# A chain of chunks in two accumulator banks, its outputs stored over its values, and two-operand GpSimd work given to other engines, in a one-core hybrid layer (RWKV-7, mLSTM, mixture of experts)

## The chip, the cores and the metric

The kernel runs on one core of a Trainium2 chip. The metric is the device time of one execution in microseconds (us). The engines are called by the profile's names: PE (TensorE matmul, with PEld for its weight loads), DVE (VectorE), ACT (ScalarE), POOL (GpSimd) and SP, which here only issues DMAs. The accumulators that PE writes lie in eight banks of 512 float32 values per partition; the program holds them as one tile, `accs`.

## The reference, cut to what matters

One decoder layer over 528 tokens (16 meta tokens and 512 others), width 1024, all in float32.

1. RMS norm of the input, then one projection to 3,080 columns.
2. Half of the heads: RWKV-7 time mixing. Per head a 64x64 state S is carried over the tokens: `S = S * d_t + (S a_t) b_t^T + v_t k_t^T`, `y_t = S r_t`. Then a norm per head, a bonus term and a gate.
3. The other half: an mLSTM, chunked over time, with a causal convolution on q and k.
4. Output projection and residual, RMS norm, a router (one of 4 groups, then 2 of its 8 experts), 32 SwiGLU experts of 1024 -> 2x512 -> 1024, residual, final RMS norm.

## The kernel before, in words

**Start (lines 505 to 640).** The transposed input `xT` arrives in eight blocks of 128 x 528. Each block is split by ACT and DVE in a high and a low part (`xh`, `xl`), so that three fast matmuls stand for one float32 matmul. The sum of squares for the first norm is made by `squares` (L613): even blocks are squared on ACT, odd ones on DVE, and POOL adds each to `acc`. Two float32 matmuls with a matrix of ones then sum `acc` over the partitions (`pss`).

**Mixing stage.** A planner (`Weave`) runs a set of Python generators, each with a rank, against a simple model of the engines' times, and so fixes the order of PE's and SP's instructions; the order of the other engines' instructions comes from the compiler. PE, like the others, takes its instructions strictly in that order. A generator can give way to another only where it has a `yield`. `projections` (L1008) is the filler with a low rank: it streams 24 weight blocks, each split in two by `prepare` (L671) and `split_block`. `heads` (L836) builds, for each of four pairs of RWKV heads, the decayed keys and queries; `products` (L902) multiplies them per chunk of 64 tokens; `inverse0` (L1357) and `inverse` (L1372) solve small triangular systems step by step (`interleaved`, L1335: one multiplication and one addition per step or half step), the first on POOL, the second on DVE.

**The chain of chunks (L1476).** Nine steps carry the RWKV state: one of 16 tokens and eight of 64. In a step, `removals` (L1421) writes `pW`, DVE copies it to `Wt`; `solved` (L1437) multiplies `Wt` by the solved system into `uv`, for each half p of the 128 partitions four matmuls and then a copy (ACT for p = 0, DVE for p = 1); `next_state` (L1446) writes `pS`, and DVE adds the decayed state, once for each p; `outputs` (L1460) writes `yv` in two groups of matmuls, the second group for each p four matmuls and then a copy by ACT into `yT`. `solved` and `outputs` hold no `yield`; the one behind `next_state` leads straight back to the chain, whose rank 0 goes before all fillers, so that the matmuls of `outputs` stand right behind those of `next_state` in PE's queue. Each of these blocks is 4 x 64 columns wide. The chain holds four banks: `pU` (banks 4 and 5: `uv` for p = 0 and `pW` in one, `uv` for p = 1 and `pS` in the other) and `pY` (banks 6 and 7: `yv` for p = 0 in one, for p = 1 in the other). All other generators share banks 0 to 3 (`every`) until the chain ends.

**After the chain.** `variances`, `gate_a` and `outputs_a` with `gated` (L1576) finish the RWKV outputs; the space of the tiles `E`, free only when the chain has ended, takes the output weights; `mixer` (L1861) does the output projection and the router. From the mark `var` on, `prefetch` (L1950) loads expert weights into whatever space is free.

**Experts (from L2040).** Sixteen pairs of experts, 12.6 MB of weights a pair, streamed by SP's queue through all free space; PE's order is written out by hand.

Of the kernel before, what the change touches and what calls it, by code (L numbers as in the profile page):

```python
# [17 lines left out]
L = 528  # L18
# [417 lines left out]
def layer(ctx, tc, a, out, dbg=None, stop=None):  # L436
# [145 lines left out]
    acc = A.get([128, L], name="acc")  # L582
# [29 lines left out]
    A.put(idle_)  # L612
    def squares(k):  # L613
        sq = A.get([128, L], name="sq") if k else acc
        if k % 2:
            V.tensor_tensor(sq, xT[:, k], xT[:, k], op=OP.mult)
        else:
            S.activation(sq, xT[:, k], AF.Square)
        if k:
            G.tensor_tensor(acc, acc, sq, op=OP.add)  # L620
            A.put(sq)

    first_block(0, 2)
    for k in range(8):
# [10 lines left out]
        if k >= 2:  # L635
            proj_k(pk1, k1h, k1l, k)
            squares(k - 2)
    for k in range(6, 8):
        squares(k)

# [27 lines left out]
    def late():  # L668
        return len(every) == 8

    def prepare(kind):  # L671

        lo_by = V if late() and kind != "q" or "P3" not in W.marks else G
# [19 lines left out]
    pss = B.get(2, "pss", rest)  # L693
    for h in range(2):
        P.matmul(pss[:, h, :264], m("ones"), acc[:, 264 * h:264 * h + 264], start=True, stop=True)
# [4 lines left out]
    A.put(xT, acc)  # L700
# [135 lines left out]
    def heads():  # L836

        for j in range(4):
# [5 lines left out]
            G.tensor_tensor(MV[:, :, 128:192], i64[:, None].to_broadcast([128, 8, 64]),  # L844
                            DT[:, j, 1:9][:, :, None].to_broadcast([128, 8, 64]), op=OP.mult)
            G.tensor_scalar(mv0[:, NM:], i64, DT[:, j, 0:1], 0.0, op0=OP.mult, op1=OP.add)
            G.tensor_tensor(nk, nk, al, op=OP.mult)
            kp = al
            S.activation(kp, al, AF.Identity, scale=c("k_a", j), bias=dv[:, 12 + j:13 + j])
            G.tensor_tensor(kp, kp, kx[j], op=OP.mult)  # L850
# [13 lines left out]
            for p in range(2):  # L864
                for i in range(2):
                    (S.copy if p else gcopy)(E[i][PAR[p], :, j, p], MV[PAR[p], 4 * i:4 * i + 4, 0:128])
            G.tensor_scalar(r[:, NM:], r[:, NM:], c("r_k", j), 0.0, op0=OP.mult, op1=OP.add)
            G.tensor_tensor(r[:, NM:], r[:, NM:], kp[:, NM:], op=OP.mult)
# [322 lines left out]
    def states():  # L1191
# [3 lines left out]
        for tb in range(-1, 3):  # L1195
# [6 lines left out]
            kw = A.get([128, 4, 64], name="kw")  # L1202
# [154 lines left out]
    def inverse0():  # L1357
# [8 lines left out]
        yield from interleaved(G, XL0, lambda s: NL0[:, s + 1:, s], NM, tm0, 99)  # L1366
# [5 lines left out]
    def inverse():  # L1372
# [39 lines left out]
        A.put(NL, XL, Y1, Y2, *tmps, *Zs)  # L1412
        dump("X", Bt)
# [23 lines left out]
    def solved(ch, first, vu, n):  # L1437
        for p in range(2):
            for j in range(4):
                o = slice(64 * p, 64 * p + n)  # L1440
                P.matmul(uv[o, p, j], (X0[PAR[p], j] if first else Bt[PAR[p], ch, j, 0:64]), Wt[PAR[p], j],
                         start=True, stop=True)
            o = slice(64 * p, 64 * p + n)
            (V.tensor_copy if p else S.copy)(vu[o, :, p], uv[o, p])
# [15 lines left out]
    def outputs(ch, vs, vu):  # L1460
        if ch % 2 == 0:
            yT.append(A.get([128, 4, 128], name="yT"))
        for j in range(4):
            for p in range(2):
                P.matmul(yv[PAR[p], p, j], vs[:, j, p], E[ch // 4][:, ch % 4, j, p, 64:128], start=(j == 0),
                         stop=False, skip_group_check=True)
        for p in range(2):
            for j in range(4):
                P.matmul(yv[PAR[p], p, j], vu[PAR[p], j, p], Bt[PAR[p], ch, j, 64:128], start=False,
                         stop=(j == 3), skip_group_check=True)  # L1470
            last = S.copy(yT[ch // 2][PAR[p], :, 64 * (ch % 2):64 * (ch % 2) + 64], yv[PAR[p], p])
# [4 lines left out]
    def chain():  # L1476
# [853 lines left out]
```

## Time and profile before

| | |
|---|---|
| median of 3 runs | 911.82 us (910.79 to 916.01) |
| the profiled execution's own time | 910.37 us |
| its span, first to last instruction | 908.5 us |
| mean granted clock of PE, share of full speed | 0.956 |
| busy: PE / DVE / ACT / POOL | 843.5 / 434.4 / 270.9 / 226.4 us |
| HBM read | 234 MB, 263 GB/s over the span |

The span is the time from the first to the last instruction on the core; the 1.9 us by which the execution's own time is longer lie around it. Busy shares are means over stages with quite different limits, so the stages have to be read one by one.

### The profile page before, as it was taken

To read this page: it belongs to the slowest core of one execution; us is meant where nothing else is said; L and a number is where in the kernel's file an instruction comes from. 1 tells how busy PE (TensorE), PEld (TensorE's weight loads), DVE (VectorE), ACT (ScalarE), POOL (GpSimd) and SP (SyncE) were. 2 spreads that over 40 slices of the span, in tenths; PEclk is the share of its full clock that TensorE was granted. 3 is DMA by queue.
4 is the path that set the end of the run, shared out by engine and by line. 5 is a ranking of instruction groups with operands and counts; after the bars stand their busy time and mean duration, and the time that the engine had idled before them with its cause. 6 is when DMAs were issued, how large, how long until landed. Compare 5 with 4: busy or idle time off the path is not lost.

```text
span 908.5 us, 13524 instructions
## 1 busy us (share of the span) xinstructions
PE 843.5 (93%) x5385; PEld 522.1 (57%) x5386; DVE 434.4 (48%) x822; ACT 270.9 (30%) x522; POOL 226.4 (25%) x297
## 2 busy tenths in 40 slices
PE   7989889879999997998899999999999999989994
PEld 5878778769999776887334444334444333323331
DVE  7676766995544668327213334233334133322324
ACT  5666555434435773333101110011101011001102
POOL 6064544464545156254100000000000000000002
PEclk8989999987999999998899999999999999999998
DMA  7201123111100137929899999999999999999982
GB/s 237 71 3 46 47 69 83 47 47 53 51 25 25 48 107 291 403 71 335 335 402 419 420 420 420 421 420 420 420 419 421 420 421 420 420 421 421 420 341 96
DMA packets 45141, 235.56 MB, mean 259 GB/s; under 512 B 9906, under 2 KB 10290, under 8 KB 21008
## 3 DMA queue, kind: packets, MB, share of 16 engines
q1 hardware_dynamic: 42192, 228.56, 63.3%
q0 software_dynamic: 2160, 3.93, 1.2%
q10 hardware_dynamic: 720, 2.15, 0.6%
q8 instruction: 44, 0.72, 0.3%
q14 instruction: 25, 0.20, 0.1%
HBM read 234.36 MB, written 4.19 MB: 263 GB/s over the span
## 4 chain that ended last, share of the span: by engine, by line
PE 53%; DMA 24%; DVE 13%; ACT 4%; issue 2%; POOL 2%; SPq 0%; ACTq 0%; DVEq 0%; POOLq 0%
PE accs L304 25%; PE accs L2070 14%; DVE arF L304 8%; DMA arF<-wgu 7%; PE accs L2115 6%; DMA arF<-wdn 5%; DMA arM<-wgu 4%; ACT arF L304 3%; PE accs L1993 2%; DMA arH<-wgu 2%; DMA arN<-wgu 2%; DMA arN<-wdn 2%; PE accs L1994 2%; DMA arF<-wo 1%; POOL arF L304 1%
## 5 line engine op out<-in xcount | busy, mean ns | idle before, releaser
L304 PE MATMUL accs<-arS,arR 128*128 128x264 f32 (+2 forms) x1136 | 184.5, 314 | 10.2 <-DVE arR L304 5.0
L304 PEld LDWEIGHTS accs<-arS,arR 128*128 128x128 f32 (+1 forms) x1136 | 162.4, 200 | 22.5 <-DVE arR L304 5.5
L304 PE MATMUL accs<-arF 64*64 64x64 f32 (+18 forms) x1223 | 127.7, 268 | 27.5 <-DVE arF L304 17.4
L1996 DVE TENSOR_TENSOR arF<-arF,accs 128x512 f32<-128x512 f32 x124 | 80.7, 681 | 98.1 <-PE accs L1994 96.6
L304 PEld LDWEIGHTS accs<-arF 128*128 128x128 f32 (+7 forms) x1202 | 102.2, 157 | 37.3 <-DVE arF L304 11.4
L2070 PE MATMUL accs<-arF 128*64 128x512 f32 x488 | 116.4, 608 | 4.2 <-DMA arF<-wgu 4.2
L304 POOL TENSOR_TENSOR arF<-arF 128x528 f32<-128x528 f32 (+13 forms) x101 | 92.3, 917 | 67.6 <-DVE arF L304 45.4
L1804 POOL DMA_INDIRECT arM<-hd,arF x15 | 15.2, 1012 | 376.2 <-DVE arF L1794 362.7
L304 DVE TENSOR_TENSOR arF<-arF 64x16 f32<-64x16 f32 (+33 forms) x183 | 89.5, 535 | 5.1 <-POOL arF L304 2.8
L2092 ACT ACTIVATE arF<-accs,arF 128x512 f32<-128x512 f32 x16 | 11.0, 687 | 247.5 <-PE accs L2070 247.5
L2070 PEld LDWEIGHTS accs<-arF 128*64 128x64 f32 x488 | 32.6, 138 | 74.2 <-issue 57.5
L304 ACT ACTIVATE arF<-arF 128x528 f32<-128x528 f32 (+8 forms) x108 | 57.9, 559 | 49.8 <-DVE arF L304 35.5
L2125 DVE SCALAR_TENSOR_TENSOR arO<-accs,arF,arO 128x1024 fp32r<-128x1024 f32 x15 | 19.3, 1283 | 103.6 <-ACT arO L2124 103.6
L304 POOL TENSOR_SCALAR arF<-arF 64x256 f32<-64x256 f32 (+9 forms) x97 | 55.3, 572 | 42.6 <-ACT arF L304 19.6
L2115 PE MATMUL accs<-arF 128*64 128x512 f32 x280 | 62.3, 595 | 0.5 <-issue 0.5
L304 ACT COPY arF<-accs 64x256 f32<-64x256 f32 (+6 forms) x119 | 43.2, 370 | 64.1 <-PE accs L304 30.5
L1993 PE MATMUL accs<-arO,OHT 128*128 128x512 f32 x124 | 57.4, 463 | 0.0
L304 DVE TENSOR_TENSOR arF<-accs,arF 128x528 f32<-128x528 f32 (+7 forms) x81 | 35.4, 460 | 34.1 <-PE accs L304 20.6
L1994 PE MATMUL accs<-arO,OHT 128*128 128x512 f32 x124 | 48.9, 394 | 0.0
L2070 PE MATMUL accs<-arN,arF 128*64 128x512 f32 x200 | 47.1, 599 | 1.6 <-DMA arN<-wgu 1.6
L304 PE MATMUL accs<-arW,arS 128*128 128x512 f32 x192 | 47.8, 406 | 0.0
L2070 PE MATMUL accs<-arM,arF 128*64 128x512 f32 x200 | 46.7, 599 | 1.0 <-DMA arM<-wgu 0.9
(141 smaller groups left out, 932.6 us busy)
## 6 DMA issues: line engine op xcount, KB each, us to landing
arF<-wgu SPq DMA_DIRECT2D x61, 1024.0 KB, 19.8
arF<-wdn SPq DMA_DIRECT2D x35, 1024.0 KB, 20.1
arN<-wgu SPq DMA_DIRECT2D x25, 1024.0 KB, 19.9
arM<-wgu SPq DMA_DIRECT2D x25, 1024.0 KB, 19.8
arH<-wgu SPq DMA_DIRECT2D x16, 1024.0 KB, 19.9
arN<-wdn SPq DMA_DIRECT2D x15, 1024.0 KB, 19.9
arF<-wb SPq DMA_DIRECT2D x23, 512.0 KB, 3.6
arH<-wdn SPq DMA_DIRECT2D x5, 1024.0 KB, 19.8
```

The lines of the kernel that those rows point to most:

```text
L304: r = f(*args, **kw)
L1804: nc.gpsimd.indirect_dma_start(out=xt[p % 2], out_offset=None, in_=hd, in_offset=bass.IndirectOffsetOnAxis(ap=idx[:, p % 2:p % 2 + 1], axi ...
L1993: P.matmul(pq, lhs, oh[:, hs], start=True, stop=False)
L1994: P.matmul(pq, lhs, ol[:, hs], start=False, stop=True)
L1996: V.tensor_tensor(hv, hv, pq, op=OP.add)
L2070: P.matmul(pgu[64 * e:64 * e + 64, h], x[:, k, 64 * e:64 * e + 64], w[:, D * e + 512 * h:D * e + 512 * h + 512], start=(k == 0), stop=(k = ...
L2092: S.activation(av, pgu[:, 0], AF.Silu, scale=r1_)
L2115: P.matmul(pdn[64 * e:64 * e + 64, h], aT[:, k, 64 * e:64 * e + 64], w[:, D * h + 512 * e:D * h + 512 * e + 512], start=(k == 0), stop=(k ...
L2125: V.scalar_tensor_tensor(ol, pdf, g1_, oh.bitcast(F32), op0=OP.mult, op1=OP.subtract)
```

## The change

- **Start.** Each block's squares go to a tile of their own, all on ACT; DVE adds them in pairs; the float32 matmul with ones sums the four pair tiles in the accumulator (8 matmuls in place of 2). POOL has no part in it.
- **`heads`.** Three POOL multiplications of two tensors for each pair of heads go to DVE; POOL's scaling of `r` and its multiplication become one DVE instruction; two POOL copies into `E` go to ACT.
- **`inverse0`** runs its steps on DVE. **`prepare`** leaves the low parts of the split weights to DVE until the inverse is done (before: until the mark `P3`, then POOL), to POOL during the chain as before, to DVE after it.
- **The chain** has two banks: `uv` of both halves and `pW` in one, `pS` and `yv` of both halves in the other. The two banks that come free go to `every` at the chain's start. `yT` lies over the values `Vs` of its two chunks.
- **After the chain**, the first multiplication of `gated` goes from POOL to DVE; the tile `sqs` becomes four; `kw`, `Gw` and `sqs` wait for space where they had to find it.
- On POOL stay: the multiplications in `valued`, `conv`, `after_o`, `next_state`'s decay `SD`, half of the output weights' splits, and the copies of `values`.

```diff
     def squares(k):
-        sq = A.get([128, L], name="sq") if k else acc
+        sqs2.append(A.get([128, L], name="sq"))
+        S.activation(sqs2[k], xT[:, k], AF.Square)
         if k % 2:
-            V.tensor_tensor(sq, xT[:, k], xT[:, k], op=OP.mult)
-        else:
-            S.activation(sq, xT[:, k], AF.Square)
-        if k:
-            G.tensor_tensor(acc, acc, sq, op=OP.add)
-            A.put(sq)
+            V.tensor_tensor(sqs2[k], sqs2[k], sqs2[k - 1], op=OP.add)
+
+    def summed(k):
+        for h in range(2):
+            P.matmul(pss[:, h, :264], m("ones"), sqs2[k][:, 264 * h:264 * h + 264], start=(k == 1), stop=(k == 7))
...
-        lo_by = V if late() and kind != "q" or "P3" not in W.marks else G
+        lo_by = V if late() and kind != "q" or "inverse" not in W.marks else G
...
-            G.tensor_tensor(MV[:, :, 128:192], i64[:, None].to_broadcast([128, 8, 64]),
+            V.tensor_tensor(MV[:, :, 128:192], i64[:, None].to_broadcast([128, 8, 64]),
                             DT[:, j, 1:9][:, :, None].to_broadcast([128, 8, 64]), op=OP.mult)
...
-            G.tensor_tensor(nk, nk, al, op=OP.mult)
+            V.tensor_tensor(nk, nk, al, op=OP.mult)
...
-            G.tensor_tensor(kp, kp, kx[j], op=OP.mult)
+            V.tensor_tensor(kp, kp, kx[j], op=OP.mult)
...
-                    (S.copy if p else gcopy)(E[i][PAR[p], :, j, p], MV[PAR[p], 4 * i:4 * i + 4, 0:128])
-            G.tensor_scalar(r[:, NM:], r[:, NM:], c("r_k", j), 0.0, op0=OP.mult, op1=OP.add)
-            G.tensor_tensor(r[:, NM:], r[:, NM:], kp[:, NM:], op=OP.mult)
+                    S.copy(E[i][PAR[p], :, j, p], MV[PAR[p], 4 * i:4 * i + 4, 0:128])
+            V.scalar_tensor_tensor(r[:, NM:], r[:, NM:], c("r_k", j), kp[:, NM:], op0=OP.mult, op1=OP.mult)
...
-        yield from interleaved(G, XL0, lambda s: NL0[:, s + 1:, s], NM, tm0, 99)
+        yield from interleaved(V, XL0, lambda s: NL0[:, s + 1:, s], NM, tm0, 99)
...
-                P.matmul(uv[o, p, j], (X0[PAR[p], j] if first else Bt[PAR[p], ch, j, 0:64]), Wt[PAR[p], j],
+                P.matmul(uv[o, j], (X0[PAR[p], j] if first else Bt[PAR[p], ch, j, 0:64]), Wt[PAR[p], j],
                          start=True, stop=True)
             o = slice(64 * p, 64 * p + n)
-            (V.tensor_copy if p else S.copy)(vu[o, :, p], uv[o, p])
+            (V.tensor_copy if p else S.copy)(vu[o, :, p], uv[o])
...
-            yT.append(A.get([128, 4, 128], name="yT"))
+            yT.append(Vs[:, ch:ch + 2].rearrange("p c j x -> p (c j x)").rearrange("p (j t) -> p j t", j=4))
...
-                P.matmul(yv[PAR[p], p, j], vs[:, j, p], E[ch // 4][:, ch % 4, j, p, 64:128], start=(j == 0),
+                P.matmul(yv[PAR[p], j], vs[:, j, p], E[ch // 4][:, ch % 4, j, p, 64:128], start=(j == 0),
...
-                P.matmul(yv[PAR[p], p, j], vu[PAR[p], j, p], Bt[PAR[p], ch, j, 64:128], start=False,
+                P.matmul(yv[PAR[p], j], vu[PAR[p], j, p], Bt[PAR[p], ch, j, 64:128], start=False,
                          stop=(j == 3), skip_group_check=True)
-            last = S.copy(yT[ch // 2][PAR[p], :, 64 * (ch % 2):64 * (ch % 2) + 64], yv[PAR[p], p])
+            last = S.copy(yT[ch // 2][PAR[p], :, 64 * (ch % 2):64 * (ch % 2) + 64], yv[PAR[p]])
...
-        pY = yield from bank(2, "pY", wide)
-        pW, pS = (pU[:, i, 256:512].rearrange("p (j x) -> p j x", j=4) for i in range(2))
-        uv = pU[:, :, 0:256].rearrange("p a (j x) -> p a j x", j=4)
-        yv = pY[:, :, 0:256].rearrange("p a (j x) -> p a j x", j=4)
+        (uv, pW), (pS, yv) = ([pU[:, i, 256 * h:256 * h + 256].rearrange("p (j x) -> p j x", j=4) for h in range(2)]
+                              for i in range(2))
         yield from until(*(f"V{j}" for j in range(4)), "P3", "X0")
+        every.extend(wide)
...
-        A.put(Vs, *VS, *VU, Wt, SD, DT)
-        Gw = A.get([128, 4, T], name="Gw")
-        sqs.append(A.get([128, 4, 4, 128], name="sq"))
-        B.put(pU, pY)
-        every.extend(rest)
+        A.put(*VS, *VU, Wt, SD, DT)
+        B.put(pU)
+        Gw, = yield from W.room(A, 1, [128, 4, T], F32, "Gw")
+        sqs.extend((yield from W.room(A, 4, [128, 4, 128], F32, "sq")))
+        every.extend(small)
...
-        G.tensor_tensor(y, y, Gw[:, :, 128 * tb:128 * tb + 128], op=OP.mult)
+        V.tensor_tensor(y, y, Gw[:, :, 128 * tb:128 * tb + 128], op=OP.mult)
```

## Rows read from the trace of the kernel before

**Rows 1.** Stages: stretch, its length, busy time by engine (count), PEclk, DMA.
```profile
50.00:165.00 115.00, 100.41 (x659) 92.43 (x659) 82.12 (x123) 65.27 (x129) 57.36 (x88) 0.94 0.19 54
165.00:194.00 29.00, 20.81 (x154) 19.79 (x152) 28.56 (x69) 9.67 (x23) 17.31 (x28) 0.93 0.18 55
194.00:225.00 31.00, 30.75 (x369) 29.50 (x370) 23.09 (x59) 13.91 (x26) 17.63 (x24) 0.72 0.08 24
225.00:300.00 75.00, 75.00 (x971) 68.80 (x970) 35.18 (x66) 32.75 (x67) 35.99 (x50) 0.96 0.12 37
300.00:351.00 51.00, 44.96 (x293) 34.56 (x290) 38.50 (x61) 34.67 (x87) 27.44 (x20) 0.99 0.32 100
656.00:861.00 205.00, 197.47 (x972) 73.99 (x970) 64.50 (x114) 20.82 (x28) 5.95 (x6) 1.00 1.01 420
```

**Rows 2.** Chain that ended last, in order of time: start, us, what.
```profile
194.25 103.05 PE accs L304 x1307
...
840.83 19.81 DMA arM<-wgu
```

**Rows 3.** Timeline of the start: start, us, engine, operation, tiles, shapes, count.
```profile
8.02 1.88 POOL L304 TENSOR_TENSOR arF<-arF 128x528 f32<-128x528 f32 x1 [4.53 <-ACT arS L304]
8.66 1.81 DVE L304 SCALAR_TENSOR_TENSOR arS<-arF,arS 128x528 fp32r<-128x528 f32 x1
17.44 0.79 DVE L304 SCALAR_TENSOR_TENSOR arS<-arF,arS 128x528 fp32r<-128x528 f32 x1
25.72 1.05 PE L304 MATMUL accs<-arF 128*128 128x264 f32 x4
```

**Rows 4.** Timeline of the inverse, 167.2 to 167.3.
```profile
167.18 2.40 POOL L304 TENSOR_TENSOR arR<-arF,arR 128x1024 fp32r<-128x1024 f32 x1 [2.43 <-ACT arR L304]
167.22 2.60 DVE L304 TENSOR_TENSOR arF<-arF 128x135 f32<-128x135 f32 x1
```

**Rows 5.** Groups by form on DVE, 0 to 230: busy, mean ns, idle before.
```profile
L304 DVE TENSOR_TENSOR arF<-arF 128x512 f32<-128x512 f32 x6 | 4.0, 686 | 0.1
L304 DVE TENSOR_TENSOR arF<-arF 128x1024 f32<-128x1024 f32 x3 | 3.7, 1222 | 0.1
L304 DVE TENSOR_TENSOR arF<-arF 128x30 f32<-128x30 f32 x4 | 0.5, 188 | 0.0
```

**Rows 6.** Groups by form on POOL, 0 to 440.
```profile
L304 POOL TENSOR_TENSOR arF<-arF 128x512 f32<-128x512 f32 x20 | 29.8, 1501 | 16.8 <-DVE arF L304 11.1 <-ACT arF L304 4.0 <-PE accs L304 1.1
L304 POOL TENSOR_TENSOR arR<-arF,arR 128x1024 fp32r<-128x1024 f32 x8 | 19.4, 2423 | 25.0 <-ACT arR L304 24.9
```

**Rows 7.** Timeline of PE: three of its waits (in brackets: idle before, releaser).
```profile
66.66 0.40 PE L304 MATMUL accs<-arF 128*128 128x192 f32 x1 [3.29 <-POOL arF L304]
194.25 0.58 PE L304 MATMUL accs<-arF 128*128 128x128 f32 x1 [6.00 <-DVE arF L304]
350.61 0.80 PE L304 MATMUL accs<-arS,arR 128*128 128x512 f32 x1 [5.03 <-DVE arR L304]
```

**Rows 8.** Timeline of DVE and ACT reading the accumulators.
```profile
74.71 0.37 ACT L304 COPY arF<-accs 64x256 f32<-64x256 f32 x1 [1.26 <-DVE arE L304]
75.11 1.41 DVE L304 TENSOR_TENSOR arE<-accs,arF 64x512 f32<-64x512 f32 x2 [0.43 <-ACT arF L304]
228.01 0.41 DVE L304 COPY arF<-accs 16x256 f32<-16x256 f32 x1 [3.02 <-PE accs L304]
228.51 0.36 ACT L304 COPY arF<-accs 16x256 f32<-16x256 f32 x1 [5.25 <-DVE arF L304]
231.60 0.36 ACT L304 COPY arF<-accs 16x256 f32<-16x256 f32 x1 [0.55 <-PE accs L304]
231.85 0.42 DVE L304 COPY arF<-accs 16x256 f32<-16x256 f32 x1 [3.43 <-PE accs L304]
```

**Rows 9.** Timeline of one step of the chain, on PE, DVE and ACT.
```profile
266.89 0.27 PE L304 MATMUL accs<-arE,arF 128*64 128x64 f32 x1
267.39 0.88 DVE L304 TENSOR_TENSOR arF<-accs,arF 64x256 f32<-64x256 f32 x2 [2.14 <-PE accs L304]
270.78 0.96 PE L304 MATMUL accs<-arF 64*64 64x64 f32 x16
271.49 0.37 ACT L304 COPY arF<-accs 64x256 f32<-64x256 f32 x1 [2.34 <-PE accs L304]
```

More of the change, by code (lines that the diff above doesn't have):

```diff
@@ L579, in layer @@
         G.memset(t, 0.0)
-    acc = A.get([128, L], name="acc")
     kh_, kl_ = kput = [A.get([128, 1024], F32R, n) for n in ("whi", "wlo")]
@@ L612, in layer @@
     A.put(idle_)
+    pss = B.get(2, "pss", rest)
+    sqs2 = []
     def squares(k):
-        sq = A.get([128, L], name="sq") if k else acc
+        sqs2.append(A.get([128, L], name="sq"))
+        S.activation(sqs2[k], xT[:, k], AF.Square)
         if k % 2:
-            V.tensor_tensor(sq, xT[:, k], xT[:, k], op=OP.mult)
-        else:
-            S.activation(sq, xT[:, k], AF.Square)
-        if k:
-            G.tensor_tensor(acc, acc, sq, op=OP.add)
-            A.put(sq)
+            V.tensor_tensor(sqs2[k], sqs2[k], sqs2[k - 1], op=OP.add)
+    def summed(k):
+        for h in range(2):
+            P.matmul(pss[:, h, :264], m("ones"), sqs2[k][:, 264 * h:264 * h + 264], start=(k == 1), stop=(k == 7))
     first_block(0, 2)
@@ L636, in layer @@
             proj_k(pk1, k1h, k1l, k)
-            squares(k - 2)
-    for k in range(6, 8):
         squares(k)
+        if k == 5:
+            summed(1)
+        if k == 7:
+            summed(3)
     W = Weave(clock, B)
@@ L668, in late @@
     def late():
-        return len(every) == 8
+        return "chain" in W.marks
     def prepare(kind):
-        lo_by = V if late() and kind != "q" or "P3" not in W.marks else G
+        lo_by = V if late() and kind != "q" or "inverse" not in W.marks else G
         if kind in "LM":
@@ L692, in layer @@
     A.put(*kput, *kput1)
-    pss = B.get(2, "pss", rest)
-    for h in range(2):
-        P.matmul(pss[:, h, :264], m("ones"), acc[:, 264 * h:264 * h + 264], start=True, stop=True)
+    summed(5)
+    summed(7)
     rstd = A.get([128, L], name="rstd")
@@ L699, in layer @@
     B.put(pss)
-    A.put(xT, acc)
+    A.put(xT, *sqs2)
     dump("rstd", rstd)
@@ L1201, in states @@
                 P.transpose(pk[:n, 128 * b:128 * b + 128], qk[2 + b][:, tk], ident)
-            kw = A.get([128, 4, 64], name="kw")
+            kw, = yield from W.room(A, 1, [128, 4, 64], F32, "kw")
             V.scalar_tensor_tensor(kw[:n], pk[:n, 0:256].rearrange("p (h x) -> p h x", h=4), 1.0 / 16,
@@ L1412, in inverse @@
         A.put(NL, XL, Y1, Y2, *tmps, *Zs)
+        W.mark("inverse")
         dump("X", Bt)
@@ L1549, in variances @@
         for tb in range(4):
-            W.add(1, variance(tb, yT[tb].rearrange(f), sqs[0][:, tb].rearrange(f)))
+            W.add(1, variance(tb, yT[tb].rearrange(f), sqs[tb].rearrange(f)))
         yield from until(*(f"var{tb}" for tb in range(4)))
-        S.activation(sqs[0], sqs[0], AF.Exp, scale=-0.5)
+        for sq in sqs:
+            S.activation(sq, sq, AF.Exp, scale=-0.5)
         W.mark("var")
@@ L1570, in outputs_a @@
             ya[tb] = yield from W.room(A, 2, [128, 4, 128], F32R, "ya", (ar_s[tb],))
-            gated(tb, sqs[0][:, tb])
+            gated(tb, sqs[tb])
             W.mark(f"ya{tb}")
             yield
-        A.put(sqs[0], BV, Gw)
+        A.put(*sqs, BV, Gw)
     def gated(tb, sq):
         y = yT[tb]
-        G.tensor_tensor(y, y, Gw[:, :, 128 * tb:128 * tb + 128], op=OP.mult)
+        V.tensor_tensor(y, y, Gw[:, :, 128 * tb:128 * tb + 128], op=OP.mult)
         V.tensor_tensor(y, y, sq, op=OP.mult)
@@ L1583, in gated @@
         V.tensor_tensor(yl, y, yh.bitcast(F32), op=OP.subtract)
-        A.put(y)
+        A.shed(Vs, 512 * tb, 512 * tb + 512)
     hp, s2 = [[] for _ in range(4)], []
```

## Prediction

> **What bounds the kernel now.** I read the table of stages first [rows 1]. From 656 on the DMA engines are full (1.01, 420 GB/s), and the chain that ended last goes there from one weight load to the next, up to the last one at 840.83 + 19.81 = 860.6 [rows 2]. That stream has a fixed volume and waits, before it runs full, for the space that the mixing stage gives back. So I take it that a mixing stage that ends x earlier or later moves the end by x: the end is decided before 435.
>
> There the reader is to see three kinds of stage. In 50 to 194 PE has gaps: 115.0 - 100.4 = 14.6 us, then 29.0 - 20.8 = 8.2, and in the second DVE is busy for 28.56 of 29 us. In 225 to 300, the chain of chunks, PE is busy 75.00 of 75.00 us: it waits for nobody, and the chain that ended last is PE alone for 103 us from 194.25 on [rows 1, 2]. In 300 to 351 PE has 6.0 us free, DVE and POOL being busy together. Whatever makes PE idle within the chain therefore lengthens it, and nothing there hides it.
>
> **Part 1: two-operand work leaves POOL.** When POOL starts a multiplication of two tensors, a DVE instruction with two tensors in SBUF stands still until it ends: at 167.18 POOL takes 2.40 us, and a DVE step of 135 elements started beside it takes 2.60 us, where one of 30 takes 0.19 and one of 512 takes 0.69 [rows 4, 5]. On POOL 512 elements cost 1.50 us and 1024 cost 2.42; on DVE 0.69 and 1.22 [rows 5, 6]. Each moved instruction costs DVE less than the stall that it removes.
>
> *Start.* A DVE instruction of 528 elements takes 1.81 us beside POOL's 1.88 and 0.79 without [rows 3]. By the code twelve such DVE instructions lie in reach of POOL's additions (four squares, eight low parts), for at most 12 x 1.0 us. But PE is near its own limit, and gets 3 more pairs of ones-matmuls at 1.05 us a pair [rows 3], 3.15 us. ACT gets four squares, for which it is idle enough. I take a gain of 3 us between 0 (PE bound at once) and 8.9 (12 less 3.15).
>
> *Heads.* For each of four j, POOL loses four products of 1.5 us, 6.0 in sequence, and DVE gets four of 0.7, 2.8 us [rows 5, 6]; the E copies go to ACT, which is busy 65 of 115 us. PE's 3.29 us at 66.66 for POOL [rows 7] should go; the other gaps in this stage are 14.6 - 3.3 = 11.3 us, and DVE and ACT, which get the work, are busy 82 and 65 of 115 us [rows 1]. Bounds 0 and 14.6; I take 4.5, the one gap and a tenth of the rest.
>
> *Inverse.* DVE gets 30 small steps of `inverse0` at no more than 0.19 us, 5.6 us, and some four splits of 1.22, 4.9 us; it loses four stalls of about 2.4, 9.6 us [rows 4 to 6], and the small stalls beside `inverse0`, each under 0.5. That nearly cancels, and the 6.00 us that PE waits at 194.25 [rows 7] largely stay. I take 2, between -1 (no small stalls counted) and 6 (that wait gone).
>
> *After the chain.* Four products of 1.5 us go to DVE at 0.69. What is late there is the split for which PE waits 5.03 us at 350.61 [rows 7]; valued products and half of the weight splits stay on POOL. I take 4, between 0 and 5.
>
> Sum of part 1: 3 + 4.5 + 2 + 4 = 13.5 us gained, between -1 and 34.5, where all four reach their ends at once; the upper half I hold for unlikely.
>
> **Part 2: the chain in two banks.** Rows 8 decide this. At 74.71 ACT copies one block out of a bank from which DVE has just read another, and it waited for DVE, 1.26 us, though no value passes between them; at 75.11 DVE waits for ACT in the same way, and their halves of the partitions differ. At 228.01 and 228.51 the two halves of `pW`, one bank, are read one after the other, the second released by DVE; at 231.60 and 231.85 the two halves of `uv`, in two banks, are read at once. The program keeps engines apart by bank, whatever the columns and partitions. Before, the chain's four banks are laid out so that PE never writes where a copy is reading. After, it does so in three places of a step:
>
> - *`solved`.* The 16 matmuls start at 270.78 and take 0.96 us; the copy of half 0 starts at 271.49 and ends at 271.86 [rows 9]. The matmuls of half 1, which start about 0.48 after the first, would have to wait for it: 1.08 - 0.48 = 0.60, and a hand-off of 0.05 (the 0.03 that ACT's end at 75.08 takes to DVE's start at 75.11 [rows 8], rounded up). 0.65 us, nine times.
> - *`outputs`, second group.* The same form with the same copy: 0.65 us, eight times.
> - *`outputs`, first group.* It now writes the bank of `pS`. Before, it starts at 266.89, right behind `next_state`; DVE's two additions out of `pS` run from 267.39 to 268.27 [rows 9]. 268.27 - 266.89 + 0.05 = 1.43 us, seven times (the last step has no `next_state`).
>
> 17 x 0.65 + 7 x 1.43 = 11.1 + 10.0 = 21.1 us. Behind each waiting matmul stands all of PE's queue, the fillers too, since no generator can come between. Copies and additions, so far uncritical, now hold PE also when they queue behind other work on engines that are busy 33 and 35 of 75 us [rows 1]: 2 us for 24 such places, a guess at 0.1 each. No row shows PE itself held back for a bank, so the lower end is 0; the upper is 25, with 24 queueings of 0.15. I take 23, as the nearest rows are of the same tile and the same kind of block.
>
> What hides it? Nothing: the chain's end releases the space for the output weights and the last gate, and PE has no gap in front of it. The two banks given to the fillers could only help if PE waited for banks, and it waits for nothing. `yT` over `Vs` moves no work; its copies wait for POOL copies issued a step earlier. The waits for space cost nothing as long as 2,048 free words are found, and the chain sheds four times that.
>
> The Trainium skill (PSUM — Partial Sum Buffer, section "PSUM bank collisions raise a hardware error") states that two engines collide only in the same bank and the same quadrant of 32 partitions, and that different quadrants of one bank may be accessed at once. By that rule the two halves of `uv` and of `yv` would not wait, and only the third place would; the rows at 74.71, 75.11 and 228.51 show this program waiting across quadrants all the same. The case is a rival below, worked out from rows.
>
> **The sum.** 910.37 (this execution's own time) - 13.5 + 23 = 919.9. The median of the runs shown, 911.82, is 1.45 us above that execution, so I say 920 for the median. 0.5% of it, 4.6 us, is about what a measurement of this kernel can tell from no change.
>
> **The rivals.**
>
> - *Only `pS` and `yv` wait*, the halves being kept apart by their partitions. 7 x 1.43 + 1 = 11 us lost; 911.8 - 13.5 + 11 = 909, or 906 with the start and the gap at 194.25 nearer to their upper ends. For it: nothing needs more. Against it: rows 8. Chance 0.12, half of it beyond 0.5%.
> - *The other side: DVE's relief decides.* If PE's gaps before 194 and at 351 go for the larger part, 22 to 25 us are gained against 21 at most; if copies are also done by the time PE comes (the planner puts fillers elsewhere), less is lost: 911.8 - 22 + 8 = 898. It wins from a gain above the 23 us of the chain. For it: DVE full in 165 to 194, and stalls of 2.4 us there. Against: the splits come back to DVE. Chance 0.15.
> - *They cancel*, or neither does what it says: the DVE relief is lost to DVE's new work and the chain's waits are half as long. Within 4.6 us of 912. Chance 0.13.
> - *PE's clock falls in the chain.* In 194 to 225, behind 6 us of idling and with matmuls of 32 columns, the granted clock was 0.72, that is at the lower level of 1.2 GHz, not 2.4, for more than half of the stretch; in the chain it was 0.96 [rows 1]. With gaps of 1.4 us among matmuls of 64 columns it may fall. If it does for a third of 75 us, half of whose work then takes twice as long, some 12 us come on top: 932. Chance 0.2.
>
> **How the numbers follow.** The forecast itself (slower by 5 to 14 us) has 0.40. Faster by over 0.5%: 0.15 + 0.06 = 0.21. Within 0.5%: 0.13 + 0.06 = 0.19. Slower: 0.40 + 0.20 = 0.60. The likeliest case alone spans 916 to 926. The range takes in most of the clock's case and of the first rival, and leaves out about the farther half of the relief's case and the worst clock: 900 to 935.
>
> **What would show it.** Step by step in the profile after: at the start DVE's instructions at 0.8 us, and PE's first projection under way some 3 us earlier; no 2.5 us DVE steps in the inverse; in the chain, PE waits of about 0.6 us named after ACT copies, two a step, and of about 1.2 us after DVE additions, one a step, and a chain longer by some 20 us between the first `pW` copy and the last; the 5 us wait at 350 gone or short. Wrong would be: a chain in which PE still waits for nobody, or a mixing stage that reaches the chain over 20 us earlier.

## The result, and the profile after

The kernel after takes 960.85 us (median of 4, 956.06 to 965.33), the kernel before, measured beside it, 911.88. The ratio is 1.0527, with a 95% interval of 1.0465 to 1.059: slower, as forecast, but by 49 us where 8 were forecast, and outside the range. The profiled execution has a span of 963.4 us (before 908.5) and a mean granted clock of 0.913 (before 0.956).

The first view is the page's table of slices, 24 us each, of after: PE's busy tenths and the tenths of full speed that its clock was granted.

```profile
PE   8889897999888878999989999999999999999994
PEclk8977999996975558999899999999999999999997
```

The reader is to see the twelfth to fifteenth slice, 265 to 361, whose clock is 7, 5, 5 and 5: that is the chain of chunks. The table of stages measures it. The columns are those of [rows 1]; the first fence is after, the second before, in the stretches that [rows 1] don't show.

```profile
0.00:225.00 225.00, 203.58 (x1477) 187.93 (x1479) 164.68 (x344) 131.11 (x233) 53.68 (x93) 0.90 0.24 76
225.00:357.00 132.00, 107.34 (x1022) 92.49 (x1019) 49.25 (x92) 40.32 (x87) 31.21 (x51) 0.68 0.07 22
357.00:488.83 131.83, 120.52 (x662) 101.41 (x663) 69.67 (x173) 58.95 (x140) 48.19 (x48) 0.90 0.55 212
```

```profile
0.00:225.00 225.00, 194.51 (x1441) 179.14 (x1443) 167.75 (x292) 119.98 (x217) 110.53 (x163) 0.90 0.22 69
300.00:434.25 134.25, 122.15 (x742) 100.48 (x739) 82.01 (x193) 63.91 (x158) 59.36 (x56) 0.94 0.59 220
```

All the loss is in the middle. The stretch that was 75 us long, without a gap and at a clock of 0.96 [rows 1], is 132 us long, with 132 - 107.3 = 24.7 us of idle PE and a clock of 0.68: of its 132 us PE spent 2 x (1 - 0.68) = 64%, 84 us, at 1.2 GHz instead of 2.4. The stage behind it is as long as before (132 and 134 us). And in the first 225 us PE is busy for 203.6 - 194.5 = 9.1 us more: POOL's relief did remove early gaps, and the planner put other work there. It didn't bring the chain forward: DVE makes the first of its eight copies of `pW` at 244.32, in before at 237.60. From that copy to the last it takes 345.20 - 244.32 = 100.9 us, in before 57.3; the prediction's sign was a chain longer by some 20 us, and it is 43.6.

The waits of one step of the chain of after, from PE's timeline, as in [rows 9]: first `solved` at full clock, then a step at the lower one.

```profile
245.85 0.68 PE L304 MATMUL accs<-arF 64*64 64x64 f32 x8
246.98 0.68 PE L304 MATMUL accs<-arF 64*64 64x64 f32 x8 [0.46 <-ACT arF L304]
...
291.99 1.12 PE L304 MATMUL accs<-arE,arF 128*64 128x64 f32 x16 [1.04 <-DVE arF L304]
293.04 1.11 PE L304 MATMUL accs<-arF 64*64 64x64 f32 x8
294.61 1.11 PE L304 MATMUL accs<-arF 64*64 64x64 f32 x8 [0.46 <-ACT arF L304]
```

The 16 matmuls of `solved` are cut in two: the second eight start 246.98 - 245.85 = 1.13 us after the first. The forecast had them start 1.13 us after it instead of 0.48, 0.65 us lost. The trace shows a gap of only 0.46: these matmuls overlap in it (192 of them in before, from 250 to 300, are listed with 224 ns each and are busy for 11.5 us together, 60 ns each), and the last one before a gap counts in full. So a wait has to be read from start to start. In the step at the lower clock the same 16 matmuls also take 1.11 us for each eight, not 0.68.

The small signs came as forecast: DVE's steps of 528 elements at the start take 790 ns on average instead of 1,316 (8 of each), and PE's wait of 5.03 us [rows 7] is gone. In the inverse no DVE step of 2.5 us is left.

### The profile page after: what moved, and what is told of

Its sections match the earlier page's. It is cut to its first block, busy times and chain, and to the rows that moved or that the text cites. A ratio compares the mean times of both kernels' runs of the same rounds, so it can differ in the third digit from the quotient of the medians.

```text
span 963.4 us, 13519 instructions
## 1 busy us (share of the span) xinstructions
PE 882.9 (92%) x5397; PEld 555.3 (58%) x5398; DVE 433.2 (45%) x880; ACT 284.6 (30%) x541; POOL 153.6 (16%) x220
## 5 line engine op out<-in xcount | busy, mean ns | idle before, releaser
L304 PE MATMUL accs<-arF 32*32 32x32 f32 (+17 forms) x1251 | 158.2, 299 | 39.0 <-ACT arF L304 28.6
L304 PE MATMUL accs<-arS,arR 128*128 128x264 f32 (+2 forms) x1136 | 187.9, 320 | 3.6 <-ACT arS L304 1.5
L304 PEld LDWEIGHTS accs<-arS,arR 128*128 128x128 f32 (+1 forms) x1136 | 166.9, 205 | 16.2 <-issue 4.6
L304 PEld LDWEIGHTS accs<-arF 128*128 128x128 f32 (+6 forms) x1230 | 127.0, 182 | 53.0 <-ACT arF L304 27.4
L2075 PE MATMUL accs<-arF 128*64 128x512 f32 x400 | 94.7, 608 | 3.5 <-DMA arF<-wgu 3.5
L304 DVE TENSOR_TENSOR arF<-arF 128x512 f32<-128x512 f32 (+32 forms) x229 | 81.6, 411 | 1.4 <-ACT arF L304 0.2
L2120 PE MATMUL accs<-arF 128*64 128x512 f32 x360 | 80.4, 595 | 1.2 <-ACT arF L2106 0.7
L304 ACT ACTIVATE arF<-arF 128x528 f32<-128x528 f32 (+6 forms) x117 | 62.3, 553 | 54.7 <-DVE arF L304 31.7
L2075 PEld LDWEIGHTS accs<-arF 128*64 128x64 f32 x400 | 26.4, 138 | 59.8 <-issue 46.5
L304 POOL TENSOR_TENSOR arF<-arF 64x256 f32<-64x256 f32 (+7 forms) x44 | 41.1, 936 | 121.7 <-DVE arF L304 96.3
L2075 PE MATMUL accs<-arN,arF 128*64 128x512 f32 x240 | 56.2, 598 | 2.2 <-DMA arN<-wgu 2.2
L2120 PEld LDWEIGHTS accs<-arF 128*64 128x64 f32 x360 | 25.3, 137 | 50.2 <-issue 40.2
```

The source lines that it names most:

```text
L304: r = f(*args, **kw)
L2075: P.matmul(pgu[64 * e:64 * e + 64, h], x[:, k, 64 * e:64 * e + 64], w[:, D * e + 512 * h:D * e + 512 * h + 512], start=(k == 0), stop=(k = ...
L2120: P.matmul(pdn[64 * e:64 * e + 64, h], aT[:, k, 64 * e:64 * e + 64], w[:, D * h + 512 * e:D * h + 512 * e + 512], start=(k == 0), stop=(k ...
```

## The experiments

"Order" below is that of PE's and SP's instructions, which the planner fixes. Where a run keeps an order, its real matmuls stand in PE's queue one by one as in the kernel named. "The router starts" is the end of PE's wait of 1.2 us for DVE behind the output projection, 416.48 in before: it tells how late the mixing stage is, without what comes behind.

**E1. Four banks.** After, with the chain's part of the diff undone but for the outputs in the values and the tiles that wait for space.

```diff
-        (uv, pW), (pS, yv) = ([pU[:, i, 256 * h:256 * h + 256].rearrange("p (j x) -> p j x", j=4) for h in range(2)]
-                              for i in range(2))
+        pY = yield from bank(2, "pY", wide)
+        pW, pS = (pU[:, i, 256:512].rearrange("p (j x) -> p j x", j=4) for i in range(2))
...
-        every.extend(wide)
```

> The kernel after with the chain's tiles in four banks again, all its other edits kept. In after the chain takes 132 us (225 to 357) at a mean granted clock of 0.68, where before took 75 us at 0.96; outside of it the two are within a few us. Theory A (the two banks make PE wait, and in the waits its clock falls): the chain is back at 65 to 80 us, mean granted clock over 0.9, time 900 to 912. Rival B (POOL's work on DVE and ACT makes the chain's copies and additions late): the chain stays over 100 us and the time over 940.

914.43 us, before 910.69, ratio 1.0045 (1.0019 to 1.0070). Theory A holds, 2.4 us over its range: the loss belongs to the banks. But the 13.5 us of gain are not there either; the router starts 4.6 us later.

**E2. Two banks alone.** After, with the edits to the start, `heads`, `inverse0`, `prepare` and `gated` undone.

> The kernel before with the two banks, the outputs in place of the values and the freed banks given to the other streams, and none of the edits that take work from GpSimd. Theory A: the whole loss is here, 955 to 975, the chain at a granted clock under 0.8 with waits of 0.46 us behind ACT copies and of 1.04 us behind DVE additions. Rival B: under 925.

947.48, ratio 1.0403 (1.0380 to 1.0425). Less than A's range, and much more than B's. The clock is 0.91 from 225 to 300 and 0.68 from 300 to 350.

**E3, "held". Two banks, two held empty.** Before, in its order; `uv` and `pW` share a bank, `pS` and `yv` another, and nobody gets the other two.

```diff
...
-        pW, pS = (pU[:, i, 256:512].rearrange("p (j x) -> p j x", j=4) for i in range(2))
...
+        pW, pS = (pt[:, 0, 256:512].rearrange("p (j x) -> p j x", j=4) for pt in (pU, pY))
+        uv, yv = (pt[:, 0, 0:256].rearrange("p (j x) -> p j x", j=4) for pt in (pU, pY))
```

> The kernel before with uv and pW in one bank and pS and yv in another, and the two banks that this frees held and left empty, so that no other stream gets a bank more. Theory A: 945 to 970, as the waits need nothing else. Rival C (the other streams, with six banks instead of four, run ahead and leave the chain without work to put between its steps): the waits alone cost their 20 to 25 us, 930 to 937, and the granted clock in the chain stays over 0.9.

944.63, ratio 1.0370 (1.0353 to 1.0388), the router 34.1 us late. Each theory was half right. The waits, with what the clock lost by them, cost this much with no new order, 0.4 us under A's range; and the clock held out for most of the chain, as C had it. The table of stages of this run:

```profile
225.00:300.00 75.00, 61.66 (x708) 54.86 (x708) 27.36 (x44) 22.42 (x46) 29.52 (x41) 0.96 0.11 32
300.00:350.00 50.00, 45.35 (x384) 37.29 (x383) 18.43 (x42) 25.19 (x50) 10.19 (x14) 0.77 0.09 29
```

And PE's waits from 225 to 335: for whom, us in total, how many, the longest.

```profile
PE accs L304 <- ACT arF L304: 10.8, 17, 1.6
PE accs L304 <- DVE arF L304: 7.2, 7, 1.0
```

17 waits behind ACT and 7 behind DVE: the 24 places of the forecast, each found. The first copy of `pW` and the last, before and then E3:

```profile
237.60 0.42 DVE L304 COPY arF<-accs 128x256 f32<-128x256 f32 x1
294.85 0.42 DVE L304 COPY arF<-accs 128x256 f32<-128x256 f32 x1 [1.11 <-PE accs L304]
```

```profile
238.25 0.41 DVE L304 COPY arF<-accs 128x256 f32<-128x256 f32 x1
321.88 0.42 DVE L304 COPY arF<-accs 128x256 f32<-128x256 f32 x1 [3.14 <-PE accs L304]
```

That is 83.6 us, where before has 57.3: 26.4 us more, where 23 were forecast.

**E4, E9, E10, E11. Filling the waits.** 62 matmuls of 128 columns that nobody reads stand in front of the places where PE waits. E4 ("filled"): in after, known to the planner, so in an order of its own; one of the two freed banks takes the fillings, and neither goes to other work. E9: after with one of the freed banks held, the control. E10: E9 with the fillings, in E9's order. E11: E3 with the fillings, in E3's order. The cut is that of E10 and E11; in E4 the call goes through the planner's handle.

```diff
+    def filled(n):
+        for _ in range(n):
+            P.engine.matmul(pF[:, 0:128], m("ones"), ident, start=True, stop=True)
...
         for p in range(2):
+            if p:
+                filled(2)
```

The last two lines stand in `solved` and in the second group of `outputs`; ahead of its first group stands `filled(4)`.

> The kernel after with 17 x 2 + 7 x 4 = 62 matmuls of 128 columns more, into a bank that nobody reads, in front of the places where PE waits in the chain: PE then has work in each wait. Theory A1 (the lower clock, not the idle time, is the larger part of the loss, and it comes from the idle time): the granted clock in the chain rises above 0.85, the chain gets shorter by 20 to 30 us, time 930 to 942. Rival A2 (the clock falls for the kind of matmuls in the chain, or it doesn't matter): the granted clock stays under 0.75 and the time is 960 to 985.

> A control: the kernel after, with one of the two banks that the chain has freed held and left empty, so that the next kernel has a bank to write and the same order of PE's real work. All theories: 950 to 966, the granted clock in the chain 0.65 to 0.8.

> The kernel of the run before this one with 62 idle matmuls of 128 columns in front of PE's waits in the chain, as in the run filled, but unknown to the kernel's own planner, so that all other matmuls stand in the same order. Theory A1 (idle time lowers the clock, and the lower clock is about half of the loss): 930 to 942, granted clock in the chain over 0.85. Rival A3 (in the run filled it was the new order that helped): 950 to 975.

> The run held, which was 944.63 with 23 us more idle time of PE between 230 and 335 than the kernel before, and at a granted clock of 0.70 to 0.84 from 300 to 350, with 62 idle matmuls in front of its waits in the chain, in the same order otherwise. Theory A1: what remains is the idle time alone, 930 to 938. Rival: the fillings cost their own time and give nothing back, 945 to 960.

Ratios to before: E4 935.85 us, 1.0269 (1.0247 to 1.0290), 25.0 us under after; E9 950.79, 1.0440 (1.0393 to 1.0486); E10 933.41, 1.0225 (1.0186 to 1.0264); E11 938.91, 1.0299 (1.0262 to 1.0335). A1 holds: work that nobody needs, in the same order, makes the kernel 950.79 - 933.41 = 17.4 us faster. The table of stages, E9, then E10:

```profile
250.00:300.00 50.00, 40.74 (x424) 35.60 (x422) 12.61 (x30) 14.47 (x31) 14.32 (x27) 0.78 0.01 2
300.00:350.00 50.00, 41.95 (x360) 34.27 (x359) 17.68 (x36) 14.70 (x41) 9.72 (x17) 0.57 0.00 1
```

```profile
250.00:300.00 50.00, 48.59 (x528) 42.05 (x525) 15.99 (x36) 16.30 (x37) 14.34 (x27) 0.97 0.01 2
300.00:350.00 50.00, 42.37 (x469) 33.91 (x469) 18.52 (x44) 29.62 (x72) 12.95 (x20) 0.96 0.08 24
```

The granted clock goes from 0.78 and 0.57 to 0.97 and 0.96. In E11, where the clock had been 0.96 and 0.77, the fillings give back only 5.7 us. With the clock repaired the three lie at about the same place: 933.4, 935.9 and 938.9, some 22 to 28 us over before. E4 and E10 lack 5.5 us that stand at the router of before and E11 (see E13), and hold the 3.7 us of E1; with both taken into account the waits cost some 24 to 28 us in all three.

Why did the clock fall in after and hardly in E3, with as much idle time? What stands between the waits differs. The groups by form on PE, 250 to 300: before, E3, after, and E1, which has the relief of after but four banks.

```profile
L304 PE MATMUL accs<-arS,arR 128*128 128x264 f32 x105 | 16.2, 306 | 0.0
```

```profile
L304 PE MATMUL accs<-arS,arR 128*128 128x264 f32 x80 | 12.5, 309 | 0.0
```

```profile
L304 PE MATMUL accs<-arS,arR 128*128 128x264 f32 x36 | 7.6, 383 | 0.0
```

```profile
L304 PE MATMUL accs<-arS,arR 128*128 128x264 f32 x48 | 7.2, 295 | 0.0
```

These are matmuls of the projections, 264 columns wide, the largest group that PE has in these 50 us of before. After has 36 of them where E3 has 80; it had done most of the others before the chain. But E1 has only 48, and its clock in the same 50 us is 0.97:

```profile
250.00:300.00 50.00, 46.59 (x692) 41.17 (x692) 27.60 (x60) 24.66 (x57) 23.00 (x43) 0.97 0.04 13
```

The same for the whole chain, from the first copy of `pW` to the last, with both shapes of these matmuls:

| | matmuls of 264 columns that start in it | PE idle, us | length, us | clock |
|---|---|---|---|---|
| before | 196 | 0 | 57.3 | 0.97 |
| E1: fewer projections | 101 | 3.4 | 55.0 | 0.97 |
| E3: the waits | 197 | 16.3 | 83.6 | 0.94 |
| E2: the waits, two banks to other work | 185 | 17.1 | 87.4 | 0.87 |
| E9: both | 101 | 15.2 | 92.6 | 0.70 |
| after: both | 101 | 19.2 | 100.9 | 0.67 |
| E10: both, waits filled | 101 | 2.6 | 76.3 | 0.98 |

So neither the waits of the two banks alone nor the missing projections alone took the clock far down here; the two together did. The orders of these runs differ in other places too, so this is as near as the runs come to it.

**E5 to E8. Pieces of the relief**, each on before with four banks: the squares; the heads; the outputs in the values with the products of `gated`; and the inverse with the outputs in the values, without which it doesn't fit.

> The kernel before with the squares alone taken from GpSimd (sums on VectorE in pairs, four pairs of matmuls with ones). The prediction gave this 3 us of gain, between 0 and 8.9. Four banks with all the other edits was 914.43, with 7 us less idle time of PE ahead of 200 and a first step of the chain that starts 8 us later. Theory D (what a piece takes out of PE's early gaps comes back as more PE work, as lower clock or as another order of the streams, so that no piece alone moves the end by more than 2 us): 909 to 913. Rival E (the pieces gain as forecast and one of them loses): 906 to 908.

> The kernel before with the four products of each head pair on VectorE and the copies into E on ScalarE. The prediction gave this 4.5 us of gain, between 0 and 14.6. Theory D: 909 to 913, though PE's gap of 3.3 us at 66 is shorter. Rival E: 904 to 908.

> The kernel before with the outputs in place of the values, with its waits for space, and with the four products with Gw on VectorE; four banks. The prediction priced the space at nothing and the products at 4 us of gain. Theory D: 909 to 913. Rival E, if this is the piece that loses: 915 to 920, PE waiting after the chain for what stands behind the space; if it gains as forecast: 906 to 908.

> The kernel before with the small inverse on VectorE and the low parts of the weights on VectorE until the inverse is done, with the outputs in place of the values (it doesn't fit without); four banks. The prediction gave the inverse 2 us of gain, between -1 and 6. Theory D: within 2 us of the run with the outputs in place of the values, PE's wait of 6.0 us at 194 gone. Rival E: 4 to 6 us under that run, or, if the low parts on VectorE are the loss, 4 us or more over it.

913.50 us, ratio 1.0014 (0.9987 to 1.0041); 912.59, 1.0011 (0.9988 to 1.0034); 913.64, 1.0031 (1.0008 to 1.0054); 915.18, 1.0045 (1.0016 to 1.0075). No piece gains: D, to within 0.6 us of its bounds; E7 and E8 are even slower, by little but clear of noise, though their traces lack 5.5 us at the router (see E13). The router starts 3.6, 2.5, 6.4 and 3.4 us late. The waits that the prediction named do go: in E6 the 3.29 us at 66.66, in E8 the 6.00 us at 194.25. What is gained there doesn't reach the end.

E8 is the piece that moves the projections. When `pW` is first copied, PE has started 925 of their matmuls in E8, 907 in after, E1, E4, E9 and E10, but 787 to 812 in before, E2, E3 and E5 to E7; and that copy comes at 244.99 in E8, 246.00 in E1, and at 235.3 to 238.3 in before, E2, E3 and E5 to E7. So the small inverse and the low parts on DVE, as the planner is told of them, put about a hundred projections ahead of the chain and start it 7 us later; the two freed banks don't (E2: 811).

E7's trace shows a place where something is lost. ACT's table loads from 290 to 440, E7 and then E13 (below), which leaves `sqs` alone; behind them PE's wait in E7:

```profile
L304 ACT ACT_TABLE_LOAD x6 | 7.7, 1283 | 0.1
```

```profile
L304 ACT ACT_TABLE_LOAD x3 | 3.8, 1283 | 0.1
```

```profile
313.84 12.19 PE L304 MATMUL accs<-arF 64*128 64x128 f32 x84 [5.33 <-ACT arF L304]
```

With `sqs` in four tiles the exponential of one tile no longer has to wait for the logarithms of all, and ACT's order alternates between the two functions, with a table load of 1.28 us at each change: six from 309 to 323, where before has three from 290 on. Two of them lie in the 5.33 us that PE waits for ACT. After has the same six, and a wait of 3.94 us behind ACT at 375. No run changes `sqs` alone, so what the loads cost at the end is not shown.

**E13, E14, E18. The relief in the order of before.** The two-operand work goes to DVE through a handle that still tells the planner "GpSimd". E13: squares' additions, heads, small inverse, low parts, `gated`; E14: without small inverse and low parts; E18: E13 with the small inverse back. Neither `sqs` nor the banks are touched; PE's order is that of before but for four matmuls with ones in the first 30 us.

```diff
+    VG = Told(nc.vector, "G", clock)
...
-            G.tensor_tensor(nk, nk, al, op=OP.mult)
+            VG.tensor_tensor(nk, nk, al, op=OP.mult)
```

> The kernel before with all the two-operand work that the change takes from GpSimd put on VectorE (the additions of the squares, the products of the heads, the small inverse, the low parts of the weights until the inverse is done, the products with Gw), the planner still told that GpSimd does it, so that PE and SP keep their order. Theory D1 (the relief is real and the new order of the streams took it back): 896 to 904. Rival D2 (the relief was never worth that much, since PE's early gaps come back later or at a lower clock): 907 to 913.

> The same without the small inverse and the low parts: only the squares, the heads and the products with Gw are on VectorE, PE and SP in the order of before. D1: 898 to 906 (of the forecast's 13.5 all but 2). D2: 907 to 913. If the inverse is what gives the gain away, this is 3 us or more under the run before it.

> The run with all the two-operand work moved in the order of before, 901.5, with the small inverse back on GpSimd. If the small inverse on VectorE is what PE waits for at 200: 896 to 900. If GpSimd's small steps stand in VectorE's way as much as they take there: 900 to 904.

E13: **901.50** us, before 912.07, ratio 0.9907 (0.9877 to 0.9936), faster than both kernels, as D1 has it. E14: 909.28, ratio 0.9982 (0.9955 to 1.0008), in D2's range; E18: 908.94, ratio 0.9970 (0.9950 to 0.9990), over both of its ranges. By the times alone the small inverse would be worth 7 us. The starts of the router, before, E13, E14 and E18:

```profile
416.48 0.65 PE L304 MATMUL accs<-arF 128*128 128x128 f32 x4 [1.20 <-DVE arF L304]
```

```profile
411.86 0.65 PE L304 MATMUL accs<-arF 128*128 128x128 f32 x4 [1.20 <-DVE arF L304]
```

```profile
411.18 0.65 PE L304 MATMUL accs<-arF 128*128 128x128 f32 x4 [1.20 <-DVE arF L304]
```

```profile
410.73 0.66 PE L304 MATMUL accs<-arF 128*128 128x128 f32 x4 [1.21 <-DVE arF L304]
```

That is 4.6 to 5.8 us earlier than before in all three: the relief is real, and the small inverse adds nothing to it. But the traced executions of E14 and E18, 904.86 and 905.10, are the fastest of their ten; by the medians the relief is worth 912.07 - 909.28 = 2.8 and 910.97 - 908.94 = 2.0 us. The first copy of `pW` comes at 234.68, 235.45 and 232.58, where before has 237.60, and 812 projections stand ahead of it as in before. E13 has the inverse on DVE as E8 has it, told to the planner as GpSimd's, and starts the chain 10 us earlier than E8. What sets E13 apart lies behind; from PE's timeline, E18 and then E13:

```profile
423.06 1.50 PE L304 MATMUL accs<-arF,arM 128*128 128x128 bf16 x24 [0.56 <-DVE arF L304]
428.63 0.46 PE L304 MATMUL accs<-arF 128*128 128x6 bf16 x12 [4.07 <-DVE arF L304]
...
429.34 12.68 PE L2072 MATMUL accs<-arF 128*64 128x512 f32 x48
```

```profile
424.67 1.50 PE L304 MATMUL accs<-arF,arM 128*128 128x128 bf16 x24 [1.28 <-DVE arF L304]
426.01 0.44 PE L304 MATMUL accs<-arF 128*128 128x6 bf16 x12
...
426.74 10.52 PE L2072 MATMUL accs<-arF 128*64 128x512 f32 x48
```

At the router's end PE either waits 4.07 us for DVE, and then runs the first 48 expert matmuls in 12.68 us, or it waits 1.28 us a little earlier where the other has 0.56, and runs them in 10.52: (4.07 + 0.56 - 1.28) + (12.68 - 10.52) = 5.5 us. During these 48 the granted clock is 0.83 in E18 and 1.00 in E13. Before and after, E1, E3, E5, E6, E11, E12, E14, E17 and E18 have the wait; E2, E4, E7 to E10, E13, E15 and E16 don't. It goes with the order that the compiler gives DVE, and no edit here aimed at it. DVE clears a tile of 128 x 2048 there, E18 and then E13:

```profile
425.49 1.76 DVE L304 MEMSET arM<- 128x2048 f32 x1 [0.38 <-issue]
```

```profile
427.06 1.76 DVE L304 MEMSET arM<- 128x2048 f32 x1 [0.38 <-PE accs L1794]
```

In all eleven traces with the wait this stands 3.1 us ahead of the matmuls that wait; in the others it stands 0.8 to 1.3 us behind their start, or (E8) 10.8 ahead. So of E13's 10.6 us some 5 are the relief and some 5.5 this.

**E15, E16, E17. One place at a time**, on before, in its order but for two matmuls and five transfers in E15.

E15 puts `pS` beside one half of `yv`, E16 both halves of `uv` in one bank, E17 both of `yv`. The line that says so is shown for each; in E16 and E17 the matmuls and copies lose the index of the half as well.

```diff
+        pW, pS = (pt[:, 0, 256:512].rearrange("p (j x) -> p j x", j=4) for pt in (pU, pY))
...
+        uv = pU[:, 0, 0:256].rearrange("p (j x) -> p j x", j=4)
...
+        yv = pY[:, 0, 0:256].rearrange("p (j x) -> p j x", j=4)
```

> The kernel before with pS in the bank of one half of yv, and nothing else changed. The waits behind VectorE's additions alone: 7 x 1.04 = 7.3 us, 917 to 920 with the clock in the chain over 0.9. If the waits of one place already take the clock down: 922 or more.

> The kernel before with both halves of uv in one bank, and nothing else changed. The waits behind ScalarE's copies alone: 9 x 0.46 = 4.1 us, 914 to 916 with the clock in the chain over 0.9. If the clock falls for these already: 918 or more.

> The kernel before with both halves of yv in one bank, and nothing else changed. By the waits alone: 8 x 0.46 to 0.5 = 4 us, 914 to 917. With the 3.3 us of pS and yv and the 11.8 us of uv this would sum to 19 us; the run with all three was 34 us over before, and the rest of that, 15 us, would be what only the three together bring, by the lower clock. If this run is over 925 instead, the places add up and nothing is left for the clock.

915.41 us, ratio 1.0052 (1.0033 to 1.0070); 923.89, 1.0155 (1.0119 to 1.0192); 921.80, 1.0118 (1.0088 to 1.0149); from 225 to 300 the clock is 0.96, 0.96 and 0.93. E15 is under its range. E16 and E17 are over the price of the waits, and E16 over the bound at which the clock was to be blamed: within the chain it is not, but from 300 to 350 it is 0.90, in before 1.00, so that some of E16's loss can be the clock's. The router starts 11.0, 14.8 and 10.6 us late, the stretch between the first and last `pW` copy is 9.0, 10.6 and 8.1 us longer. That adds up: 36.4 against 34.1 us at E3's router, 27.7 against 26.4 in its chain. (E15 and E16 lack the router's 5.5 us.) In E15 the third place can be read whole:

```profile
241.71 0.97 PE L304 MATMUL accs<-arF 128*64 128x64 f32 x16
243.71 0.69 PE L304 MATMUL accs<-arE,arF 128*64 128x64 f32 x16 [1.04 <-DVE arF L304]
```

`outputs` starts 2.00 us after `next_state`, before 0.57 (266.32 to 266.89 [rows 9]): 1.43 us, the forecast's number. The waits behind ACT come to more than 0.65: nine in E16 with gaps of 6.9 us in sum, some of 0.98 and one of 1.6, where ACT is busy with something else when the block is ready.

**E12. Filling before's own gaps** with 70 such matmuls, in its order.

> The kernel before, with 70 idle matmuls of 128 columns in six of its own gaps (11 ahead of the wait at 66.7, 9 at 124.5, 6 at 163, 7 at 171.3, 20 at 194.3 and 17 at 350.6), all else in the same order. In before the clock is at its lower level for 3 to 7 us after five of these, some 20 us in all, which at half speed cost up to 10 us. Theory A1: those spells are gone and the time is 901 to 907. Rival F (PE isn't what sets the end there, or the spells don't come from the gaps): 909 to 914.

916.59, ratio 1.0053 (1.0020 to 1.0085): over both ranges, and it settles nothing. PE's order was kept; in DVE's, which the compiler makes, some instructions changed places. The wait behind the fillings is still there, and another one is new:

```profile
185.37 4.63 PE L311 MATMUL accs<-arF 128*128 128x128 f32 x40
195.52 2.62 PE L313 MATMUL accs<-arF 128*128 128x128 f32 x10 [5.52 <-DVE arF L313]
...
216.00 1.33 PE L313 MATMUL accs<-arF 128*128 128x128 f32 x5 [6.23 <-ACT arF L313]
```

## Why the direction was right and the size wrong

- **What bounds the kernel**: right. What the mixing stage loses arrives at the end: E3's router is 34.1 us late and E3 33.9 slower, E17's 10.6 and 10.8; E15 and E16 agree to within 2.5 us once the router's 5.5 are added.
- **Part 2, the waits**: right in place, number and size. 24 waits of 0.65 and 1.43 us were forecast and found; the queueing was 26.4 - 21.1 = 5.3 us rather than 2. 23 us forecast, 26.4 in E3's chain, and 24 to 28 in the runs with the waits filled. The rival that only `pS` and `yv` wait falls with E16 and E17: E17, in which only the two halves of `yv` share a bank, is 921.8 against 911.0, with eight waits of PE behind ACT's copy. The Trainium skill (PSUM — Partial Sum Buffer, section "PSUM bank collisions raise a hardware error") states that two engines may use one bank at the same time in different quadrants of 32 partitions. By that rule E17, whose halves have 64 partitions each, would be at 911. The program's semaphores order the accesses here, so no run shows what the hardware would have done.
- **"Sum of part 1: 3 + 4.5 + 2 + 4 = 13.5 us gained"**: the first step that failed. Each term was worked out with the order of before. In that order the relief is worth 2 to 5 us (E13, E14, E18), within the bounds, at less than half the value taken. Told of the other engines, the planner makes another order, in which nothing is left of it: with four banks the kernel is 3.7 us slower (E1), and the step is 17 us off. For the inverse E8 and E13 show it, the planner told and not told of the same work: the first `pW` copy comes at 244.99 and at 234.68 (E13 has the work of the start and of the heads on DVE besides; by E14 that is worth 2.2 us at this place). E5 and E6 point the same way, but there the work differs too (six more matmuls with ones in E5, copies moved to ACT in E6). The four tiles in place of `sqs`, for which no term stood in the sum, bring three more table loads on ACT and PE waits behind them (E7); their share is not shown.
- **The clock in the chain**: the second. It was a rival, with a chance of 0.2 and 12 us, as if a third of 75 us ran at the lower clock, and was no term of the sum. It was 84 us of 132, and the runs put its price at 17.4 us (E9 to E10). After to E4 it is 25.0, but 5.5 of these are the router's wait, which E4 lacks, and E4's order and banks are others. Waits and clock are not independent: the clock fell where the waits met an order with little wide work left, since the new order had put the projections ahead of the chain (E8). With the order of before its price was 5.7 us (E3 to E11).
- Together: 911.9 + 3.7 (E1) + 26.9 (E4 over E1, the router's 5.5 added to E4) + 19.5 (after over E4, likewise) = 962.0; measured 960.85. Each term is the difference of two runs, and the last one ends in after itself, so the sum shows the sizes and is no test of them.
- A slip in the forecast's last step: 919.9 is for the traced execution, and the 1.45 us by which the median lies over it give 921.3, not 920. It changes nothing here.
- Open: why the planner starts the chain later when it is told that DVE has the small inverse, and which of the relief's other pieces make up E1's 3.7 us.

## What to carry to other kernels

Where a planner or a compiler draws up the order anew, price an edit twice: in the old order (here by telling the planner nothing: 2 to 5 us gained) and with the new one (here 3.7 us lost). Before tiles share an accumulator bank in a serial chain, count from start to start what each reader holds up, and ask what wide work is left to stand in the gaps: here the clock cost 17 us on top of some 26 for the waits. A tile cut in pieces to fit can set free an order that the whole tile had forbidden.

## What the runs showed that was not expected

- Matmuls that nobody reads made the kernel 17.4 us faster (E9 to E10), by the clock that PE was granted over 100 us.
- The same kind of wait, at the same idle share (39.6 and 40.9 of 50 us busy), left the clock at 0.98 in E3 and 0.74 in after, from 250 to 300; the missing projections with four banks left it at 0.97 (E1).
- One order of DVE's work at the router costs 5.5 us, a wait and the lower clock behind it, and comes and goes with edits 100 us away. A comparison of 1% in this kernel has to look there first.
- E14 and E18 spread over 904.86 to 914.63 and 905.10 to 911.72 us in ten executions each, E13 over 900.91 to 903.56 in five; what makes the difference was not found.
